# A conditioned decoder layer on one Trainium2 core: projections and copies reordered, a sort counted in two rows, and sums sent from the rows they end in

## The chip, the cores and the metric

The kernel runs on one core of a Trainium2 chip. Its time is the device time of the whole program in microseconds (us). Most runs of one kernel agree within 0.3%. The engines of a core work side by side, each through its own queue in order: TensorE (PE: matmuls, and PEld: the loading of their stationary operands), VectorE (DVE), ScalarE (ACT), GpSimd (POOL), and SyncE (SP), which here only starts DMA transfers. ACT and POOL also start transfers, and an engine that waits for a transfer or for another engine holds up all that is behind it in its queue.

## The reference

One layer of a decoder, run for a prompt of 512 tokens and for 8 samples of 8 tokens (64 tokens), 576 tokens of 2048 channels in all:

```python
h  = RMSNorm(x) * (1 + scale1) + shift1            # scales, shifts and gates from silu(c) @ w_ada
x_lru, y_gate, B, C, x_sc = split(h @ W_in)        # 5 x 1024 channels
a  = RGLRU(causal_conv4(x_lru)) * gelu(y_gate)     # recurrent scan, 16 heads of 64
b  = B * causal_conv3(C * x_sc)
x  = x + gate1 * (concat(rmsnorm(a), rmsnorm(b)) @ W_out)
h2 = RMSNorm(x) * (1 + scale2) + shift2
# PEER: 8 heads, 128 x 128 product keys, the best 16 of 16384 experts for each head
out[t] = sum over heads and picks of w * gelu(h2[t] . expert_u[e]) * expert_v[e]
x  = x + gate2 * out;   y = RMSNorm(x)
```

Outputs are y for both groups and the new states of the scan and of the two convolutions. All inputs are fp32.

## The kernel before

A product of two fp32 matrices is made of three matmuls of a rounded high part and a low remainder (`hi*hi`, `hi*lo`, `lo*hi`): the high part is written by ACT (`whi`, `xhi`, `hhi`), the low part by POOL or DVE (`wlo`, `xlo`, `hlo`).

First come the modulation and the first norm, then `project`, which streams a block of 128 output channels of a weight matrix in two halves of 8 x 128 rows and runs 96 matmuls of 288 tokens. The LRU loop goes over 8 channel groups: `lru_gate(i, 0)` and `lru_gate(i, 1)` are the small gate matmuls (`pg`), `lru` the scan. The products of the slices of `w_ada` that are needed later are put between as `ada_turn`. A second loop makes the projections c, s and b of the short convolution. `norm_stats` takes a norm: squares are summed by DVE (`sqa`), added over partitions by TensorE (`pc_g`), a root is taken by ACT and DVE (`rc`), and spread to all partitions by TensorE (`st_g`); the function it returns gives R. Then 16 projections with `w_out`, which read all of `hv`, the normed channels.

For h2, four quarters of four channel blocks are modulated, multiplied with the first block of the queries' weights (`qa`), transposed into a wide PSUM tile (`wide`, L609), and copied by ACT to `h2s` (L612); SP sends them to `h2d` in DRAM.

PEER is done in two ways at once. Experts that are picked by many tokens are computed densely: a list of 84 blocks of 128 experts is streamed, first `ut` (the U stream, 168 pieces of 24 matmuls, `pu`) and then `v` (the V stream, 84 steps of four columns, `pv`). Their activations weigh with a table that `gbank` matmuls build piece by piece from outer products of pairs (`op`, `wr`) that DVE and ACT make. Tokens that have many picks outside of the list are sorted by DVE and TensorE into tiles (`SORTED`: first position, 64 or 128 tokens, number of rows) with the samples' group 0 ahead. For each tile, rows of expert_u and expert_v are gathered by indirect DMAs that POOL starts (L1147), DVE takes dot products in the U stream (L1175), and adds rows times weights in the V stream into `accB` in PSUM (L1201). A tile of 64 tokens has two picks of each token beside each other, one on partitions 0 to 63 and one on 64 to 127, so its sum has two halves. ACT copies the sum to a new row buffer (L1205), and POOL adds it to `accd` in DRAM by one indirect DMA for 128 tokens or two, the second adding to the first, for 64 (L1210).

A planner in Python writes the order of the queues: before each piece, `ahead` takes steps of the generators as far as a credit in microseconds allows (a `yield 4.0` is a step that costs 4.0), and `LAG` says how many pieces behind the tile's rows its next stage begins. Row buffers are handed out by `new_row`, six in the V stream, in rotation. In the V stream each step's weights are split by ACT (L843) and POOL (L844). `finish_b` ends the samples' part: it reads their sums from `accd` (`tokb`), transposes them with 32 matmuls (`ph`, L1378), and writes y; `fplan` names the columns of the V stream between which its steps stand. At the end the four blocks of prompt tokens are read from `accd` (`tok`) and added by matmuls to the last group's sums.

Of the kernel before, what the change touches and what calls it, by code (L numbers as in the profile page):

```python
# [49 lines left out]
FULL_ROWS = 1.25  # L50
LAG = 2
PAIRS = 6
# [25 lines left out]
def build(ctx, tc, A, O, dbg=None):  # L78
# [36 lines left out]
    def stream_w(src, nm, share=8):  # L115
        his, los = [], []
        for hf in range(2):
            raw = ws.tile([128, 8, 128], F32, name=f"raw_{nm}_{hf}", tag="wraw", bufs=2)
            nc.sync.dma_start(raw, src[:, 8 * hf:8 * hf + 8, :])
            hi = ws.tile([128, 8, 128], F32R, name=f"whi_{nm}_{hf}", tag="whi", bufs=2)  # L120
            S.activation(hi, raw, AF.Copy)
            lo = ws.tile([128, 8, 128], F32R, name=f"wlo_{nm}_{hf}", tag="wlo", bufs=2)
            lo_engine(share).tensor_sub(lo, raw, r32(hi))
            his.append(hi)
            los.append(lo)
        return his, los

    def mm3(outs, his, los, movs, ks=range(KD)):
# [427 lines left out]
    R = spread()  # L556
# [46 lines left out]
    for q in range(4):  # L603
        modulate(x1, R, 4, 3, 4 * q, 4, "h2")
        mm3(pq0, *w_q, movs, range(4 * q, 4 * q + 4))
        for i in range(NA // 128):
            for k in range(4):
                for p in range(2):
                    PE.matmul(wide[:, i, k * 128:(k + 1) * 128], hv[p][:, 4 * q + k, i * 128:(i + 1) * 128], idr,  # L609
                              start=p == 0, stop=p == 1)  # L610
        t = adap.tile([128, 4, 512], F32, name=f"h2s{q}", tag="wa")
        S.activation(t, wide, AF.Copy)  # L612
        for i in range(NA // 128):
# [31 lines left out]
    actd = dr.tile([L, 128, NA], F32, name="actd")  # L645
    accd = dr.tile([T, D], F32, name="accd")
    x2d = dr.tile([128, KD, NA], F32, name="x2d")
# [116 lines left out]
    slot_of, row_log, slots_now = {}, [], [RB]  # L764

    def new_row(nm):

        k = len(row_log)
        s_ = slot_of[k] = (slot_of.get(k - 1, -1) + 1) % slots_now[0]
        row_log.append(False)  # L770
        return (gp if s_ < RB else pools["vx"]).tile([128, D], F32, name=nm, tag=f"row{s_}", bufs=1), k

    def row_free():

        s_ = (slot_of.get(len(row_log) - 1, -1) + 1) % slots_now[0]
        return all(row_log[k] for k in range(max(0, len(row_log) - 2 * RV), len(row_log)) if slot_of[k] == s_)

# [240 lines left out]
    def sort():  # L1018
# [12 lines left out]
        rk = pools["rsort"].tile([128, QT], F32, name="rk")  # L1031
        hot = []

        def count_up():
            for out, lhs, rhs, first, last in hot:
                PE.matmul(out, lhs, rhs, start=first, stop=last)  # L1036
            hot.clear()

        for z in range(QT):
# [3 lines left out]
            V.tensor_scalar(oh, io, rk[:, z:z + 1], None, op0=ALU.is_equal)  # L1043
            todo_ = []
            for i, (p0, n, c) in enumerate(GT):
                if p0 is None:
                    continue
                lhs = oh[:, p0:p0 + n]
                if n < 128:
                    lhs = pools["rsort"].tile([128, 128], F32, name=f"ohd{i}_{z}", tag="ohd", bufs=4)  # L1050
                    V.tensor_copy(lhs.rearrange("p (r t) -> p r t", t=n),
                                  oh[:, None, p0:p0 + n].to_broadcast([128, 2, n]))
                todo_.append((pt[:, 2 * i:2 * i + 2], lhs, m[:, 0:2, z], z == 0 and i == 1,
                              z == QT - 1 and i == len(GT) - 1))
            count_up()
            hot.extend(todo_)
            yield 4.0
        yield None
        count_up()
        srt = pools["rsort"].tile([128, len(GT), 2], F32, name="sorted")  # L1060
# [123 lines left out]
    def gather_v(i):  # L1184
# [7 lines left out]
        def add(j):  # L1192
            r, a = held.pop(j)
            row_log[a] = True
            if j == 0:
# [4 lines left out]
                return  # L1200
            V.scalar_tensor_tensor(st["a"], r, dots[i][:, j:j + 1], st["a"], op0=ALU.mult, op1=ALU.add)  # L1201

        def end():
            t, a = new_row(f"acc{i}")
            S.activation(t, st["a"], AF.Copy)  # L1205

            def out():
                row_log[a] = True
                for o in range(0, 128, n):
                    G.indirect_dma_start(out=accd, out_offset=bass.IndirectOffsetOnAxis(ap=tok[:n, i:i + 1], axis=0),  # L1210
                                         in_=t[o:o + n], in_offset=None, compute_op=ALU.add if o else ALU.bypass)
            after.append([gu[0] + 3, out])

        for j in range(c):
            fetches.append(lambda j=j: fetch(j))
            uses.append(lambda j=j: (add(j), end() if j == c - 1 else None))

# [150 lines left out]
    def finish_b():  # L1368

        r = new_row("tokb")[0]  # L1370
        nc.sync.dma_start(r[:NG], accd[NA:T, :])
        xt = new_row("x2b")[0]
# [4 lines left out]
        for k in range(KD):  # L1377
            PE.matmul(ph[:, k * NG:(k + 1) * NG], r[:NG, k * 128:(k + 1) * 128], ident[:NG, :NG], start=True, stop=True)  # L1378
        V.tensor_tensor(s4(t), s4(ph[:, :KD * NG].rearrange("p (k t) -> p k t", k=KD)), ctx_b(g2, slice(0, KD)), op=ALU.mult)
# [433 lines left out]
```

## Time and profile before

| what | value |
|---|---|
| median of 3 runs | 3400.45 us (3397.44 to 3406.22) |
| profiled execution | 3398.16 us, its span 3396.0 us |
| TensorE busy | 3183.6 us, 94% of the span |
| TensorE's mean granted clock | 0.963 of full speed |
| DVE, ACT, POOL busy | 2155.1, 1084.6, 1739.4 us |
| moved by DMA | 868.17 MB, mean 256 GB/s |
| stages, by the trace | LRU loop to 380 us, short convolution to 729, w_out to 970, h2 and queries to 1236, U stream to 2336, V stream 2346 to 3366 |

A row of the timeline gives the start, the duration, the engine, the line of the kernel, the operation, output and inputs with shapes, and in brackets how long the engine sat idle before it and what ended this. A row of the waits gives the engine and the group that waited, what it waited for, the total, how often, and the longest. Matmuls are pipelined, so one lasts longer than the distance to the next.

### The profile page before, as it was taken

The numbers are of one execution on the slowest core, as the hardware profiler recorded it, in microseconds if no ns is written. First come the engines' busy times: TensorE is split into PE (matmuls) and PEld (weight loads), VectorE is DVE, ScalarE is ACT, GpSimd is POOL, SyncE is SP. The second block draws the span as 40 slices with busy tenths as digits, with TensorE's granted clock in tenths as the row PEclk, the third lists the DMA queues.
The fourth block names the chain that finished last, engine by engine and source line by source line (L and its number), as shares of the span: only waits on it lengthen the run. The fifth ranks groups of instructions, "written<-read, shape, count | busy, mean of one in ns | idle before, by whom it ended". The sixth has DMA issues, their size and how long they took to land.

```text
span 3396.0 us, 47497 instructions
## 1 busy us (share of the span) xinstructions
PE 3183.6 (94%) x17641; PEld 2699.9 (80%) x17641; DVE 2155.1 (63%) x3246; ACT 1084.6 (32%) x1665; POOL 1739.4 (51%) x993
## 2 busy tenths in 40 slices
PE   5899999989979999998999999998999999899987
PEld 2588789889969998877888888876887777687776
DVE  5355522243346898877788986755666777677735
ACT  3244211132232222223555555532322222222122
POOL 4233233344333246664565665655766676666732
PEclk8899999999979999999999999998999999999998
DMA  9643456633432228986979898988999988898954
GB/s 338 230 143 132 164 200 214 211 120 130 136 137 71 69 94 285 313 301 240 352 278 373 336 355 324 357 326 337 374 365 330 355 312 295 304 361 295 361 160 148
DMA packets 304030, 868.17 MB, mean 256 GB/s; under 512 B 36618, under 2 KB 80522, under 8 KB 255658
## 3 DMA queue, kind: packets, MB, share of 16 engines
q1 hardware_dynamic: 165152, 390.35, 33.6%
q0 software_dynamic: 62896, 386.64, 29.4%
q10 hardware_dynamic: 75744, 88.09, 7.4%
q8 instruction: 139, 2.28, 0.3%
q14 instruction: 99, 0.81, 0.1%
HBM read 864.69 MB, written 68.90 MB: 275 GB/s over the span
## 4 chain that ended last, share of the span: by engine, by line
PE 51%; DMA 4%; issue 4%; DVE 2%; POOL 2%; ACT 0%; POOLq 0%; SPq 0%; ACTq 0%; DVEq 0%
PE pu L1295 24%; PE pv L1315 23%; PE gbank L1491 3%; DMA v<-v,rows 2%; POOL xlo L844 1%; DMA u<-u,rows 1%; POOL v L1147 1%; PE pv L1319 0%; DMA tok<-accd 0%; DMA raw<-v 0%; DVE kk L1115 0%; DVE acc L1677 0%; DMA h2r<-h2d,tok 0%; PE tokp L1036 0%; PE ph L1378 0%
## 5 line engine op out<-in xcount | busy, mean ns | idle before, releaser
L844 POOL TENSOR_TENSOR xlo<-raw,xhi 128x1024 fp32r<-128x1024 f32 x336 | 821.3, 2457 | 647.8 <-ACT xhi L843 642.9
L843 ACT ACTIVATE xhi<-raw 128x1024 fp32r<-128x1024 f32 x336 | 354.7, 1060 | 858.4 <-PE pv L1315 429.1
L1201 DVE SCALAR_TENSOR_TENSOR accB<-v,dots,accB 128x2048 f32<-128x2048 f32 x205 | 482.3, 2353 | 187.8 <-DMA v<-v,rows 184.9
L1175 DVE SCALAR_TENSOR_TENSOR u<-u,hT 128x2048 f32<-128x2048 f32 x211 | 477.9, 2284 | 189.8 <-DMA u<-u,rows 172.8
L1315 PE MATMUL pv<-ahi,xhi 128*128 128x512 f32 x1344 | 538.4, 401 | 22.6 <-DVE acc L1337 13.3
L1315 PE MATMUL pv<-ahi,xlo 128*128 128x512 f32 x1344 | 535.8, 399 | 23.2 <-POOL xlo L844 23.2
L1295 PE MATMUL pu<-hhi,xhi 128*128 128x512 f32 x1344 | 541.9, 403 | 2.2 <-ACT xhi L843 2.2
L1315 PE MATMUL pv<-alo,xhi 128*128 128x512 f32 x1344 | 532.5, 396 | 0.0
L1295 PE MATMUL pu<-hhi,xlo 128*128 128x512 f32 x1344 | 529.0, 394 | 2.2 <-POOL xlo L844 2.2
L1295 PE MATMUL pu<-hlo,xhi 128*128 128x512 f32 x1344 | 530.6, 395 | 0.0
L1315 PEld LDWEIGHTS pv<-ahi,xlo 128*128 128x128 f32 x1344 | 256.0, 191 | 87.2 <-POOL xlo L844 27.6
L1315 PEld LDWEIGHTS pv<-ahi,xhi 128*128 128x128 f32 x1344 | 256.3, 191 | 84.3 <-ACT xhi L843 15.4
L1315 PEld LDWEIGHTS pv<-alo,xhi 128*128 128x128 f32 x1344 | 256.4, 191 | 58.0
L1295 PEld LDWEIGHTS pu<-hhi,xlo 128*128 128x128 f32 x1344 | 254.1, 189 | 60.3 <-POOL xlo L844 3.1
L1295 PEld LDWEIGHTS pu<-hhi,xhi 128*128 128x128 f32 x1344 | 255.2, 190 | 54.8 <-ACT xhi L843 2.6
L1295 PEld LDWEIGHTS pu<-hlo,xhi 128*128 128x128 f32 x1344 | 254.8, 190 | 50.1
L1147 POOL DMA_INDIRECT v<-v,rows x211 | 240.9, 1142 | 60.2 <-issue 38.0
L1147 POOL DMA_INDIRECT u<-u,rows x211 | 216.1, 1024 | 72.1 <-DVE u L1175 33.8
L1491 PEld LDWEIGHTS gbank<-wr,op 128*128 128x128 f32 x1024 | 135.5, 194 | 30.6 <-ACT op L1485 14.1
L1485 ACT ACTIVATE op<-op,it 128x128 f32<-128x128 f32 x512 | 154.5, 390 | 15.1 <-DVE op L1477 15.1
L186 PE MATMUL ada<-wa,cpad 128*32 128x512 f32 x768 | 114.6, 701 | 41.5 <-DMA wa<-w_ada 41.4
L1491 PE MATMUL gbank<-wr,op 128*128 128x84 f32 x1024 | 132.7, 273 | 18.0 <-ACT op L1485 13.3
(477 smaller groups left out, 5491.4 us busy)
## 6 DMA issues: line engine op xcount, KB each, us to landing
wa<-w_ada SPq DMA_DIRECT2D x96, 1024.0 KB
raw<-ut SPq DMA_DIRECT2D x168, 512.0 KB
raw<-v SPq DMA_DIRECT2D x336, 256.0 KB
actd<-act ACTq DMA_DIRECT2D x84, 256.0 KB
gd<-stg ACTq DMA_DIRECT2D x64, 336.0 KB
actr<-actd ACTq DMA_DIRECT2D x21, 1024.0 KB
gsb<-gd ACTq DMA_DIRECT2D x21, 1024.0 KB
raw_o<-w_out SPq DMA_DIRECT2D x32, 512.0 KB
```

The costliest lines, as they stand in the source:

```text
L186: PE.matmul(acc[32 * g:32 * g + 32, :], cpad[:, 4 * kq + g, :], w[:, g, :], start=kq == 0, stop=kq == 3)
L843: S.activation(hi, raw, AF.Copy)
L844: G.tensor_sub(lo, raw, r32(hi))
L1147: G.indirect_dma_start(out=out, out_offset=None, in_=src, in_offset=bass.IndirectOffsetOnAxis(ap=idx, axis=0), bounds_check=NE * 128 - 1, ...
L1175: V.scalar_tensor_tensor(r, r, 1.0, st["h"], op0=ALU.mult, op1=ALU.mult, accum_out=dots[i][:, j:j + 1])
L1201: V.scalar_tensor_tensor(st["a"], r, dots[i][:, j:j + 1], st["a"], op0=ALU.mult, op1=ALU.add)
L1295: PE.matmul(pu, st[:, kk, :], movA[mv](k), start=k == 0 and a == 0, stop=k == KD - 1 and a == 2)
L1315: PE.matmul(pv, st, mv, start=first and j == 0 and a == 0, stop=last and not end and j == SG - 1 and a == 2)
L1485: S.activation(ops[:, j0 + j, :], ops[:, j0 + j, :], AF.Copy, scale=it[2][:, b * 4 + j:b * 4 + j + 1])
L1491: PE.matmul(pg[:, j * L:(j + 1) * L], ops[:, j0 + j, :], wr[:, j0 + j, :], start=True, stop=True)
```

## The change

- In the last round of the LRU loop an `ada_turn` and the first c projection stand between the two gate matmuls. In the second loop the s projection stands ahead of the norm's matmuls.
- `out_half` runs one half of a w_out projection. The first halves of the first two stand ahead of the second norm's sum and between that and its spread; the other halves come where the projections were.
- The copy of `wide` is in two halves, each at high priority as soon as two blocks are transposed.
- In the sort, counts are made as two rows of 512 positions, by one matmul for each block of 128 tokens with a two-column stationary operand, copied by ACT (`two`), and turned by small matmuls into `tokq`. The step's cost for the planner is 1.3 instead of 4.0.
- `LAG` is 3 instead of 2.
- `free_slot` gives the row that has been free for longest, in place of a rotation.
- The last addition of a tile writes its sum over the last gathered row; ACT's copy and its row go. Group 0 goes as one plain DMA of 128 rows to `accs`. Of the others, the first part is sent two uses later and the second half of a 64-token tile four further uses later.
- `finish_b` reads `accs` and adds the two halves in its matmuls by `both`, the sum of the two halves of the identity. Its steps stand later in the V stream.

```diff
-LAG = 2
+LAG = 3
...
+        else:
+            ada_turn(1)
+            pc0 = project(A["w_in"][24], "c0")
         lru_gate(i, 1)
         lru(i)
         gate(i)
-        ada_turn(1)
+        if i + 1 < KW:
+            ada_turn(1)
...
-        sc_c(i, project(A["w_in"][24 + i], f"c{i}"))
+        sc_c(i, project(A["w_in"][24 + i], f"c{i}") if i else pc0)
+        ada_turn(2)
+        sc_x(i, project(A["w_in"][32 + i], f"s{i}"))
         if i == 0:
             spread = norm_stats(st, W, "g0")
...
-        sc_x(i, project(A["w_in"][32 + i], f"s{i}"))
-        ada_turn(2)
...
+    def out_half(k, hf):
+        hi, lo = half_w(A["w_out"][k], f"o{k}", hf)
+        mm3([p_out[k][:, i, :HT] for i in range(2)], (hi, hi), (lo, lo), movs, range(8 * hf, 8 * hf + 8))
+
+    p_out = [pp.tile([128, 2, 512], F32, name=f"pp_o{k}", tag="pp") for k in range(2)]
+    out_half(0, 0)
     spread = norm_stats(st, W, "g1")
+    out_half(1, 0)
     ada_turn(2)
     R = spread()
...
-            p = project(A["w_out"][k], f"o{k}")
+        if k < 2:
+            out_half(k, 1)
+            p = p_out[k]
+        else:
+            p = project(A["w_out"][k], f"o{k}")
...
-        S.activation(t, wide, AF.Copy)
+            if i % 2:
+                with tc.high_priority():
+                    S.activation(t[:, i - 1:i + 1, :], wide[:, i - 1:i + 1, :], AF.Copy)
...
+    def free_slot():
+
+        free = [(held_by.get(s_, -1), s_) for s_ in range(slots_now[0]) if s_ not in held_by or row_log[held_by[s_]]]
+        return min(free)[1] if free else None
...
-            yield 4.0
+            last_oh.append(oh)
+            yield 1.3
+            if z:
+                PE.matmul(pt[0:2, :], m[:, 0:2, z - 1], last_oh[z - 1], start=z == 1, stop=False)
         yield None
-        count_up()
+        PE.matmul(pt[0:2, :], m[:, 0:2, QT - 1], last_oh[QT - 1], start=False, stop=True)
+        two = pools["rsort"].tile([2, NA], F32, name="two")
+        S.activation(two, pt[0:2, :], AF.Copy)
+        yield None
+        pt = pbank("g", "tokq", 2)
+        for i, (p0, n, c) in enumerate(GT):
+            for o in range(0, 128 if i else 0, n):
+                PE.matmul(pt[o:o + n, 2 * i:2 * i + 2], two[:, p0:p0 + n], ident[0:2, 0:2], start=True, stop=True)
...
-        def end():
-            t, a = new_row(f"acc{i}")
-            S.activation(t, st["a"], AF.Copy)
...
-            after.append([gu[0] + 3, out])
+            V.scalar_tensor_tensor(r, r, dots[i][:, j:j + 1], st["a"], op0=ALU.mult, op1=ALU.add)
+            row_log[a] = False
+
+            if not i:
+                after.append([gu[0] + 2, lambda: (row_log.__setitem__(a, True), G.dma_start(accs, r))])
+                return
+
+            def out(o):
+                row_log[a] = o + n == 128
+                G.indirect_dma_start(out=accd, out_offset=bass.IndirectOffsetOnAxis(ap=tok[:n, i:i + 1], axis=0),
+                                     in_=r[o:o + n], in_offset=None, compute_op=ALU.add if o else ALU.bypass)
+            for o in range(0, 128, n):
+                after.append([gu[0] + 2 + 4 * (o > 0), lambda o=o: out(o)])
...
-        nc.sync.dma_start(r[:NG], accd[NA:T, :])
+        nc.sync.dma_start(r, accs)
+        both = vp.tile([128, NG], F32, name="both")
+        V.tensor_add(both, ident[:, :NG], ident[:, NG:])
...
-            PE.matmul(ph[:, k * NG:(k + 1) * NG], r[:NG, k * 128:(k + 1) * 128], ident[:NG, :NG], start=True, stop=True)
+            PE.matmul(ph[:, k * NG:(k + 1) * NG], r[:, k * 128:(k + 1) * 128], both, start=True, stop=True)
...
-    fplan = {(last + 1, 2), (last + 2, 0), (last + 2, 2), (last + 2, 3), (last + 3, 1), (last + 3, 3)}
+    fplan = {(last + 1, 2), (last + 2, 3), (last + 3, 1), (last + 3, 3), (last + 4, 1), (last + 4, 3)}
```

More of the change, by code (lines that the diff above doesn't have):

```diff
@@ L115, in stream_w, with half_w @@
     def stream_w(src, nm, share=8):
[L116 to L125, printed above, removed]
-        return his, los
+        his, los = zip(*[half_w(src, nm, hf, share) for hf in range(2)])
+        return his, los
+    def half_w(src, nm, hf, share=8):
+        raw = ws.tile([128, 8, 128], F32, name=f"raw_{nm}_{hf}", tag="wraw", bufs=2)
+        nc.sync.dma_start(raw, src[:, 8 * hf:8 * hf + 8, :])
+        hi = ws.tile([128, 8, 128], F32R, name=f"whi_{nm}_{hf}", tag="whi", bufs=2)
+        S.activation(hi, raw, AF.Copy)
+        lo = ws.tile([128, 8, 128], F32R, name=f"wlo_{nm}_{hf}", tag="wlo", bufs=2)
+        lo_engine(share).tensor_sub(lo, raw, r32(hi))
+        return hi, lo
     def mm3(outs, his, los, movs, ks=range(KD)):
@@ L605, in build @@
         mm3(pq0, *w_q, movs, range(4 * q, 4 * q + 4))
+        t = adap.tile([128, 4, 512], F32, name=f"h2s{q}", tag="wa")
         for i in range(NA // 128):
@@ L645, in build @@
     actd = dr.tile([L, 128, NA], F32, name="actd")
-    accd = dr.tile([T, D], F32, name="accd")
+    accd = dr.tile([NA, D], F32, name="accd")
+    accs = dr.tile([128, D], F32, name="accs")
     x2d = dr.tile([128, KD, NA], F32, name="x2d")
@@ L773, in row_free @@
     def row_free():
-        s_ = (slot_of.get(len(row_log) - 1, -1) + 1) % slots_now[0]
-        return all(row_log[k] for k in range(max(0, len(row_log) - 2 * RV), len(row_log)) if slot_of[k] == s_)
+        return free_slot() is not None
     for i in range(RB):
@@ L1031, in sort @@
         rk = pools["rsort"].tile([128, QT], F32, name="rk")
[L1032 to L1037, printed above, removed]
+        last_oh = []
         for z in range(QT):
@@ L1200, in add @@
                 return
[L1201 to L1212 removed]
+            if j < c - 1:
+                V.scalar_tensor_tensor(st["a"], r, dots[i][:, j:j + 1], st["a"], op0=ALU.mult, op1=ALU.add)
+                return
[3 more added lines that the diff above has]
+                after.append([gu[0] + 2, lambda: (row_log.__setitem__(a, True), G.dma_start(accs, r))])
+                return
+            def out(o):
[4 more added lines that the diff above has]
+                after.append([gu[0] + 2 + 4 * (o > 0), lambda o=o: out(o)])
         for j in range(c):
             fetches.append(lambda j=j: fetch(j))
[L1216 removed]
+            uses.append(lambda j=j: add(j))
     UO = range(len(GT))
```

22 lines of the change are left out of this document (5 added, 17 removed).

## The prediction

> **What bounds the kernel now.** I read the page first, then the chain, the waits of TensorE, and the timeline of POOL, DVE and ACT around each of those waits.
>
> ```profile
> span 3396.0 us, 47497 instructions
> PE 3183.6 (94%) x17641; PEld 2699.9 (80%) x17641; DVE 2155.1 (63%) x3246; ACT 1084.6 (32%) x1665; POOL 1739.4 (51%) x993
> PEclk8899999999979999999999999998999999999998
> PE 51%; DMA 4%; issue 4%; DVE 2%; POOL 2%; ACT 0%; POOLq 0%; SPq 0%; ACTq 0%; DVEq 0%
> ```
>
> TensorE is busy for 94% of the span and holds most of the chain that names an engine. The change removes almost no matmul work, so it can win only what TensorE does not use: the idle 3396.0 - 3183.6 = 212.4 us, and the slow matmuls behind each hole, where the granted clock falls. The waits say which holes there are (total, count, longest):
>
> ```profile
> PE pv L1315 <- POOL xlo L844: 23.2, 8, 7.8
> PE gbank L1491 <- ACT op L1485: 13.3, 2, 9.3
> PE pv L1315 <- DVE acc L1337: 13.3, 9, 3.0
> PE pc_g L225 <- DVE sqa_g L217: 8.7, 2, 6.9
> PE wide L609 <- ACT h2s L612: 8.6, 1, 8.6
> PE tokp L1036 <- issue: 7.7, 1, 7.7
> PE ph L1378 <- DMA tokb<-accd: 6.7, 1, 6.7
> ```
>
> The change touches all seven, each in whole or in part.
>
> **V stream: sums written into their rows, halves of 64-token tiles apart, oldest free row.** This is half of the forecast. Timeline of POOL and TensorE around three sums, and one undisturbed window (its columns: length, PE busy and count, PEld, DVE, ACT, POOL, granted clock, DMA share, GB/s):
>
> ```profile
> 2606.01 1.87 POOL L1210 DMA_INDIRECT accd<-acc,tok  x1 [9.47 <-DMA accd<-acc,tok]
> 2633.88 0.80 PE L1315 MATMUL pv<-ahi,xhi 128*128 128x512 f32 x1 [3.04 <-DVE acc L1337]
> 2925.77 4.76 POOL L844 TENSOR_TENSOR xlo<-raw,xhi 128x1024 fp32r<-128x1024 f32 x2 [8.66 <-ACT xhi L843]
> 2933.28 0.93 POOL L1210 DMA_INDIRECT accd<-acc,tok  x1 [0.30 <-issue]
> 2944.46 1.47 POOL L1210 DMA_INDIRECT accd<-acc,tok  x1 [10.26 <-DMA accd<-acc,tok]
> 2948.36 0.80 PE L1315 MATMUL pv<-ahi,xlo 128*128 128x512 f32 x1 [7.80 <-POOL xlo L844]
> 2953.92 0.39 PE L1315 MATMUL pv<-ahi,xhi 128*128 128x512 f32 x1
> 3133.95 1.48 POOL L1210 DMA_INDIRECT accd<-acc,tok  x1 [10.67 <-DMA accd<-acc,tok]
> 3137.87 0.79 PE L1315 MATMUL pv<-ahi,xlo 128*128 128x512 f32 x1 [7.30 <-POOL xlo L844]
> 3158.78 0.50 PE L1315 MATMUL pv<-ahi,xhi 128*128 128x512 f32 x1 [0.68 <-DVE acc L1337]
> 2960.00:3130.00 170.00, 168.24 (x729) 136.36 (x728) 138.98 (x84) 41.00 (x37) 115.66 (x70) 1.00 0.93 344
> ```
>
> POOL issues the second half of a tile right behind the first, and sits some 10 us until the first has landed (it must: the second adds to the same rows). Its queue holds the next xlo, which TensorE wants. At 2948.36 that costs TensorE 7.80 us; then thirteen matmuls take 2953.92 - 2948.36 = 5.56 us where 168.24 / 729 = 0.231 us each would be 3.00, so 2.6 more: 10.4. The same reading gives 7.30 + about 2 = 9.3 at 3137.87, and 3.04 + about 3 = 6 at 2633.88, where POOL's lost time came out as late rows for DVE. Small waits just behind the three (0.4 to 1.9 us, eight of them, the last is the row at 3158.78) add about 6. Together 31.7 us.
>
> With the change the two halves are four uses of rows apart; in the built order one xlo pair and four fetches lie between: 4.76 + 4 x 1.3 (a fetch of 1.00 and its 0.30 of issue) = 10 us, against 2944.46 - 2933.28 = 11.2 us to land. So 1.2 us of 10.3 is left, at two tiles. The third stall, group 0, becomes one plain 128-row transfer with nothing behind it. POOL loses no instruction otherwise; ACT loses six copies, which lay beside TensorE: nothing. What is late next: the sum's row is now the oldest free one, so it is taken by the first or second fetch behind its transfer, and that fetch waits until it is read out: 11.2 - 1.0 - 4.76 = 5.4 us at most at the two 64-token tiles, up to 4 at the others. POOL has slack for that: it waited 8.66 us for xhi before its pair at 2925.77, so it runs ahead of TensorE there. I charge 3 us over all six sums (bounds 0 and 12: six times 2). Net +28.7, from 19 to 33.
>
> The Trainium skill, TensorE: Matmul & The Clock Gate, Part 1, says that after an idle window of about 3.4 us the array runs at half speed for about 3.4 us of busy time. Here the slow stretch behind the 7.80 us hole was 5.3 us or more; by the page each of three such holes would be worth about 1 us less, and the term about 26. The measurement decides.
>
> **End: finish_b later.**
>
> ```profile
> 3259.84 7.08 PE L1378 MATMUL ph<-ident,tokb 64*128 64x64 f32 x32 [6.68 <-DMA tokb<-accd]
> ```
>
> It now reads accs, written 600 us earlier instead of just now, so its 6.68 us go. The 32 instructions run at 7.08 / 32 = 0.22 us in the slow clock; at the full clock half, 3.5 us, and the V matmuls behind them are no longer slow (about 1). The stationary grows from 64 to 128 rows at the same moving width: nothing. The add that makes `both` is one small DVE instruction, beside other work. +11 (7 to 14). The last scatter is later used only by the four tok loads, as before.
>
> **First stages.** Timeline of TensorE, DVE and ACT, and a window of the h2 stage:
>
> ```profile
> 356.57 1.23 PE L432 MATMUL pg<-xc,g_lru_wa 64*64 64x300 f32 x8 [0.98 <-ACT ti L433]
> 362.88 2.27 PE L432 MATMUL pg<-xc,g_lru_wx 64*64 64x300 f32 x8 [5.08 <-ACT tr L433]
> 366.71 0.53 PE L136 MATMUL pp_c<-hhi,whi_c 128*128 128x288 f32 x2
> 379.32 0.43 PE L136 MATMUL pp_c<-hhi,wlo_c 128*128 128x288 f32 x2
> 381.55 1.28 PE L225 MATMUL pc_g<-ones,sqa_g 128*128 128x1 f32 x10 [1.80 <-DVE sqa_g L217]
> 735.53 2.26 PE L225 MATMUL pc_g<-ones,sqa_g 128*128 128x1 f32 x10 [6.85 <-DVE sqa_g L217]
> 742.16 2.28 DVE L558 SCALAR_TENSOR_TENSOR o<-o,cols,R_g 128x576 f32<-128x576 f32 x3 [2.91 <-ACT R_g L237]
> 754.02 2.62 DVE L243 TENSOR_TENSOR hlo<-o,hhi 128x576 fp32r<-128x576 f32 x2
> 990.46 0.48 PE L609 MATMUL wide<-idr,hhi 128*128 128x128 f32 x1 [8.65 <-ACT h2s L612]
> 1014.83 0.53 PE L136 MATMUL wide<-hhi,whi_q 128*128 128x288 f32 x1 [2.02 <-ACT h2s L612]
> 981.80:1018.40 36.60, 25.94 (x160) 25.79 (x160) 8.64 (x10) 13.57 (x13) 17.14 (x11) 0.72 0.41 144
> ```
>
> Last LRU round. A projection takes 379.32 + 0.43 - 366.71 = 13.0 us. c0 and an ada turn now lie in the 5.08 us wait; s0 takes c0's old place ahead of the norm and covers, as c0 did, the chain of 381.55 - 365.15 = 16.4 us from the last gate matmul to the squares. Gained: 5.08, the slow gate matmuls (2.27 against 1.23, so 1.04) and about 2 of the slow ada and st_g matmuls behind; the 1.80 stays. +8 (5 to 10).
>
> out_half. The first half of w_out[0], 6.5 us, fills the 6.85 us at 735.53. That of w_out[1] goes between pc_g and st_g, so R comes later, by about 6.5 less the two holes of 1.5 us and less slow clock: some 2.5 us, 742.16 to 744.7. From R, DVE with its helpers needs 754.02 + 2.62 - 742.16 = 14.5 us for the last eight chunks; the second half of o0 trickles behind them to about 760, and o1 ends near 766, where two whole projections from 744 with their waits ended it at about 770. The hole moves behind st_g rather than going: +3.5 (-1 to +7).
>
> h2 copies. The window has 10.7 us idle and a clock of 0.72. Half a copy now goes early on ACT; the other half still stands behind five of the next quarter's activations, so only the first half of quarter 1's transposes gets ahead of its wait, 2 to 3 us; each later quarter finds its copy done, the slow matmuls between 990 and 1002 shrink by about 2, and the 2.02 becomes about 1. +6 (0 to 10). SP sends the same h2d transfers; one weight load moves between two halves of them, read some 10 us later: nothing.
>
> **Sort and LAG.** Rows of the group view (min/median/max ns), of DVE, ACT and TensorE:
>
> ```profile
> L1036 PE MATMUL tokp<-nd_m,ohs x24: 251/353/353, 1524.0 to 1538.0; 128*128 128x2 f32 x24
> L1036 PE MATMUL tokp<-nd_m,ohd x16: 167/353/354, 1523.5 to 1538.2; 128*128 128x2 f32 x16
> 1564.78 0.83 DVE L1082 TENSOR_SCALAR sl<-R 128x128 uint32<-128x128 uint32 x1
> 1581.54 0.28 DVE L1115 MATCH_REPLACE8 kk<-sl,kk 128x128 f32<-128x128 f32 x1
> 1583.92 1.98 PE L1491 MATMUL gbank<-wr,op 128*128 128x84 f32 x8 [9.30 <-ACT op L1485]
> 1655.95 1.88 ACT L1162 ACTIVATE hT<-h2r 128x2048 f32<-128x2048 f32 x1 [10.41 <-DMA h2r<-h2d,tok]
> ```
>
> The counts took 40 small matmuls, about 40 x 0.19 = 7.6 us (they overlap by half). Now four with 512 moving columns: the gate row above moves 8 x 300 columns in 1.23 us, so 8 passes of 512 take 2.1, and seven transposes, about 3 to 4 in all. The 7.7 us wait for the first count stays: it is DVE's chain, and the first one-hot row comes no earlier. Eight copies go from DVE, one short copy comes to ACT: nothing. +1.5 (-2 to +4).
>
> The smaller cost told to the planner (1.3 for 4.0 of each count) and LAG 3 move DVE's work. Before, the lump of 1564.78 to 1581.82 (17.0 us, the first tile's top-k) ends just ahead of the pairs that gbank needs, and TensorE waits 9.30. In the built order the lump runs a piece later with the second tile's first steps behind it, about 28 us (the same instructions at the same durations, 17.0 + 11), and the first gbank one and a half pieces later. TensorE then reaches gbank three pieces of 5.5 = 16.5 us behind the lump's issue; the pairs are there after 3 for the row sums ahead, 28 and 2.1 (1583.92 - 1581.82): a wait of some 16.5, 7 worse. Against that, the second tile's h2r is fetched a piece ahead: ACT's 10.41 us at 1655.95, which holds xhi and lengthens two pieces by 5.0 and 2.1 (estimated from the starts of the U pieces), goes: 7 better. Net 0 (-10 to +8).
>
> **Sum.** V 28.7 + end 11 + LRU 8 + out_half 3.5 + h2 6 + sort 1.5 + U 0 = 58.7 us. The profiled execution took 3398.16 us (2.16 around its span), so 3339.5; the median of the runs shown, 3400.45, is 2.3 above it: **3342 us**.
>
> **The rivals.**
>
> DVE's lump decides (U). The wait at the first gbank is 20 to 30 us and the second tile's head start is used up by DVE, 63% busy over all and late for a few pieces. For it: 9.30 us waited there with a lump of 17.0. Against: the excess is DVE's, and pieces without sort work have DVE to spare. Loss 25 to 30 instead of 0: about 3370.
>
> The POOL wait moves instead of going. The fetch into the sum's row sits out the transfer, and the second half finds the first unfinished. For it: 11.2 us to land against 10 of work between, and in the built order the first fetch behind a 64-token tile's second half takes that very row. Against: the 8.66 us that POOL had in hand. If two thirds of the 31.7 come back: 3342 + 21 = 3363.
>
> The Trainium skill, DMA: Bandwidth & Descriptors, Rules for kernel authors, says of an accumulating DMA beside another access of the same bytes that one must wait for the earlier DMA's semaphore. The row at 2944.46 shows that wait; by this rule it cannot be dropped, only covered, and where the cover is short this rival holds.
>
> Slower: the same wait at all six sums, uncovered. Place: POOL, at the fetch behind each sum. Price: 10.4 us of TensorE each, as at 2948.36, and 2 of small waits: 6 x 12.4 = 74 against the 31.7 removed, 42 worse. With 11 + 8 + 3.5 + 6 + 1.5 = 30 from the other places and U at its bad end of -10: 3400 + 42 - 20 = 3422. It decides when more than four of the six sums stall in full ((31.7 + 20) / 12.4 = 4.2).
>
> The change does little. TensorE idles elsewhere for the same total: DMA, at a share of 0.93 in the undisturbed V window, has no more to give, and rows come late: 3392.
>
> **How the numbers follow.** Forecast 0.62, with its own range 3317 to 3362 (terms' ends, not all at once); the lump 0.12; the wait that moves 0.13; little 0.05; slower 0.08. The range 3315 to 3388 takes in the first three and leaves the last two and a few hundredths below. 0.3% of the time, 10 us, is what a measurement can tell: faster 0.87, same 0.05, slower 0.08.
>
> **What would show it.** In the waits of TensorE: xlo from 23.2 to under 10 in the V stream, no tokb wait, no 5.08 and no 6.85; h2s at 5 or less. At POOL: no wait of 9 us at a scatter, at the fetch behind it under 5. The first gbank's wait near 16 us, and the ACT wait for h2r gone. The prediction is wrong if POOL shows six waits of 8 us or more at v fetches with TensorE's waits behind them, if DVE's rows come late through several U pieces, or if V pieces still take their time with the DMA share at 1.

## The result, and the profile after

The changed kernel takes 3363.26 us (median of 4 runs, 3360.20 to 3368.04) against 3402.20 us: the ratio is 0.9887, with a 95% interval from 0.9867 to 0.9907. It is faster by 38.9 us, clear of the 10 us that a measurement can tell. The forecast was 58 us. The profiled execution took 3366.13 us, 32.0 less than the one before.

The page of the changed kernel:

```profile
span 3364.0 us, 47459 instructions
PE 3182.0 (95%) x17623; PEld 2695.6 (80%) x17623; DVE 2150.7 (64%) x3239; ACT 1077.9 (32%) x1666; POOL 1732.3 (51%) x992
PEclk8899999999989999998999999998999999999998
PE 49%; DMA 9%; issue 2%; DVE 2%; POOL 1%; ACT 0%; SPq 0%; POOLq 0%; DVEq 0%; ACTq 0%
```

TensorE was busy as long as before (3182.0 us against 3183.6): between these two profiles nearly all of the gain is idle time, as argued. Against a second profile of the kernel before (3188.1 us busy of 3398.8), 28.7 of the 34.8 us are idle time. The waits of TensorE in the changed kernel, those that answer to the ones shown before, and the new ones:

```profile
PE pv L1333 <- DVE acc L1355: 16.3, 8, 4.4
PE gbank L1511 <- ACT op L1505: 13.9, 1, 13.9
PE wide L626 <- ACT h2s L630: 8.8, 5, 4.1
PE tokp L1064 <- issue: 7.4, 1, 7.4
PE pv L1333 <- POOL xlo L867: 5.1, 3, 3.2
PE pp_o L136 <- ACT hhi L242: 3.9, 2, 3.6
PE st_g L233 <- DVE rc_g L146: 2.7, 1, 2.7
```

The V stream's wait for xlo went from 23.2 to 5.1 us; what is left stands at its start, between 2344 and 2365 us, none of it behind a sum. The wait for tokb (6.7) is gone, and the one for the squares fell from 8.7 to 0.4. But h2s still costs 8.8 us, in five parts, and DVE's acc rose from 13.3 to 16.3. One more wait shrank that no term of the prediction names, the one of the first V matmul, here before and after:

```profile
PE pv L1315 <- ACT xhi L843: 9.2, 1, 9.2
```

```profile
PE pv L1333 <- ACT xhi L866: 3.7, 1, 3.7
```

ACT's `xhi` stood behind its `ahi`, and that behind DVE's `actr`. Before, DVE waited for the activations to come back from DRAM; after, it did not. Why the transfer was in time is open. DVE before and after:

```profile
2340.68 2.29 DVE L1258 TENSOR_TENSOR actr<-actr,gsb 128x2048 f32<-128x2048 f32 x1 [5.67 <-DMA actr<-actd]
```

```profile
2336.95 2.28 DVE L1276 TENSOR_TENSOR actr<-actr,gsb 128x2048 f32<-128x2048 f32 x1
```

To see where the time went, the span is cut at starts of TensorE's groups. Each length is worked out from the first (or last) instruction of a group in the trace; `before` has two profiles, since the kernel was profiled again, and the last column holds the other runs whose code is the changed one in that stretch.

| stretch | before | changed | others like the changed |
|---|---|---|---|
| first gate matmul to end of the last b projection | 559.8, 560.2 | 554.2 | 552.6 to 555.4 |
| to the second norm's sum (all of w_out) | 221.2, 227.3 | 221.6 | 221.6 |
| first query matmul to first whole query projection (h2) | 45.2, 44.9 | 46.3 | 46.2 to 46.5 |
| to the U stream | 222.5, 222.4 | 223.8 | 223.5 to 224.0 |
| U stream, to the first V matmul | 1108.6, 1107.5 | 1106.9 | 1104.2 to 1109.5 |
| V stream, to the samples' matmuls (ph) | 913.9, 911.8 | 899.2 | 887.2 to 898.2 |
| ph to the last V matmul | 109.8, 111.7 | 95.9 | 95.4 to 97.9 |
| first V matmul to the 3696th | 906.9, 904.9 | 890.7 | 878.6 to 889.6 |
| from there to the last V matmul | 116.8, 118.6 | 104.5 | 103.9 to 106.4 |

The two rows that meet at ph do not hold the same work before and after: before, 3696 V matmuls stand ahead of ph and the first row ends with the 6.7 us wait for tokb; in the changed kernel 3732 do. The last two rows are cut at the same V matmul, so the gains of the V stream and of the end are read from them. Seven profiles share the V stream's code of the changed kernel (the changed one, and the six others in the row to the 3696th); they spread over 12 us, with a mean of 885.4, so a single profile tells little that is smaller. Below, "the V stream" is the row up to ph; among the changed kernel and those made from it that row holds the same work.

### The profile page after: what moved, and what is told of

Read it like the earlier page. It is cut to its first block, busy times and chain, and to the rows that moved or that the text cites. A ratio compares the mean times of both kernels' runs of the same rounds, so it can differ in the third digit from the quotient of the medians.

```text
span 3364.0 us, 47459 instructions
## 1 busy us (share of the span) xinstructions
PE 3182.0 (95%) x17623; PEld 2695.6 (80%) x17623; DVE 2150.7 (64%) x3239; ACT 1077.9 (32%) x1666; POOL 1732.3 (51%) x992
## 4 chain that ended last, share of the span: by engine, by line
PE 49%; DMA 9%; issue 2%; DVE 2%; POOL 1%; ACT 0%; SPq 0%; POOLq 0%; DVEq 0%; ACTq 0%
PE pu L1313 25%; PE pv L1333 20%; PE gbank L1511 3%; DMA gsb<-gd 2%; DMA v<-v,rows 2%; DMA actr<-actd 2%; DMA raw<-v 1%; DMA h2r<-h2d,tok 1%; POOL xlo L867 1%; PE pv L1337 0%; DMA tok<-accd 0%; DVE kk L1129 0%; DVE acc L1697 0%; DVE accB L1216 0%; POOL v L1161 0%
## 5 line engine op out<-in xcount | busy, mean ns | idle before, releaser
L1216 DVE SCALAR_TENSOR_TENSOR accB<-v,dots,accB 128x2048 f32<-128x2048 f32 x199 | 468.2, 2353 | 155.9 <-DMA v<-v,rows 149.0
L1333 PE MATMUL pv<-ahi,xhi 128*128 128x512 f32 x1344 | 536.8, 399 | 22.8 <-DVE acc L1355 16.3
L1355 DVE TENSOR_TENSOR acc<-acc,pv 128x512 f32<-128x512 f32 x144 | 96.8, 682 | 88.7 <-PE pv L1333 86.0
```

What stands on the lines that cost most here:

```text
L1333: PE.matmul(pv, st, mv, start=first and j == 0 and a == 0, stop=last and not end and j == SG - 1 and a == 2)
L1355: V.tensor_add(ak, ak, pv)
```

## The experiments

**Early half projections, and the pace of w_out.** In the first pair of profiles w_out looked as if out_half had won nothing (221.2 and 221.6 us), although o1 ended earlier: all later projections took 12.80 us instead of 12.48. So out_half was undone.

```diff
-    out_half(0, 0)
-    out_half(1, 0)
...
-        if k < 2:
-            out_half(k, 1)
-            p = p_out[k]
-        else:
-            p = project(A["w_out"][k], f"o{k}")
+        p = project(A["w_out"][k], f"o{k}")
```

> The changed kernel with the two early half projections undone, so that all 16 w_out projections run whole behind the norm. In the trace of the changed kernel the stretch from the last b projection's end to the second norm's sum (pc_n) takes 221.7 us against 221.2 before, although o1 ends 4.0 us earlier by that clock: the 14 projections behind it run at 12.80 us each instead of 12.48. Theory: the way the stream of w_out starts sets its pace (0.1300 or 0.1333 us a matmul) for all that follows without a hole. Then here it is 12.48 again and the stretch about 221 us. Rival: the pace is drawn anew in every execution, or belongs to other parts of the change; then 12.80 stays and the stretch takes 225 to 226 us.

It took 3370.67 us, at 12.80 us a projection: the rival's pace. The stretch took 227.3 us, a little beyond the rival's 225 to 226. Whether the pace belongs to other code or to the execution was left to two more runs. The kernel before, with only a comment added, profiled once more:

> The kernel before, profiled once more. Its first profile runs 15 projections of w_out at 0.1300 us a matmul (221.2 us from the last b projection to the norm); the same code in the run with only the later parts changed ran at 0.1333 (226.1 us). Theory: the pace is drawn by the execution; it may be 0.1300 or 0.1333 here, and 0.1333 (about 226 us) shows it. Rival: it belongs to the code of before; then 0.1300 and 221 us again. The V stream up to ph took 913.9 us: theory of the V holes, 910 to 918 again.

It took 3400.98 us. w_out ran at the slower pace, 227.3 us, and the V stream took 911.8 us. The window from 800 to 900 us, all of it w_out's matmuls (columns: length, PE busy and count, PEld, DVE, ACT, POOL, granted clock, DMA share, GB/s), first of the kernel before, then of the same kernel again:

```profile
800.00:900.00 100.00, 100.00 (x772) 100.00 (x771) 33.98 (x47) 27.38 (x32) 40.45 (x18) 1.00 0.41 133
```

```profile
800.00:900.00 100.00, 100.00 (x752) 100.00 (x751) 30.84 (x44) 26.82 (x32) 39.40 (x18) 1.00 0.41 132
```

The same code, the same granted clock and DMA load, and 772 against 752 recorded matmuls. So the pace does not belong to the code; whether the execution or the device it ran on sets it, the runs do not show. The profile that the prediction was made from had the fast one, 5 to 6 us better in this stretch than the others. Against the usual pace out_half won 227.3 - 221.6 = 5.7 us.

**The halves of the wide copy.** One copy for each quarter, as before:

```diff
-            if i % 2:
-                with tc.high_priority():
-                    S.activation(t[:, i - 1:i + 1, :], wide[:, i - 1:i + 1, :], AF.Copy)
+        S.activation(t, wide, AF.Copy)
```

> The changed kernel with one copy of the wide tile for each quarter, as before. From the first query matmul to the first whole projection the stage took 45.2 us before and 46.3 after. Theory: the halves cost about a microsecond, since the transposes of the second half wait for the copy of the first (4.1 us at the first quarter); here 45 us. Rival: the early copies help and something else in the changed kernel (the modulation, DMA) made the stage longer; then 48 us or more here.

The stage took 44.6 us and the stretch behind it 222.1, where the changed kernel has 46.3 and 223.8. The halves cost 1.7 us in each, about 3 together: the theory, with more than its one microsecond. The whole took 3363.21 us. The other way round, the second two blocks went to PSUM banks of their own and were copied one by one:

```diff
+        gs = [pbank("g", f"wg{q}_{i}", 2) for i in range(2)]
+        dst = [wide[:, 0, :], wide[:, 1, :], gs[0], gs[1]]
...
-                    PE.matmul(wide[:, i, k * 128:(k + 1) * 128], hv[p][:, 4 * q + k, i * 128:(i + 1) * 128], idr,
+                    PE.matmul(dst[i][:, k * 128:(k + 1) * 128], hv[p][:, 4 * q + k, i * 128:(i + 1) * 128], idr,
...
-            if i % 2:
+            if i:
                 with tc.high_priority():
-                    S.activation(t[:, i - 1:i + 1, :], wide[:, i - 1:i + 1, :], AF.Copy)
+                    S.activation(*((t[:, 0:2, :], wide[:, 0:2, :]) if i == 1 else (t[:, i, :], dst[i])), AF.Copy)
```

> The changed kernel with the transposes of blocks 2 and 3 written to two other PSUM banks, each a tile of its own, copied by itself as soon as it is full; blocks 0 and 1 stay in the wide tile. Theory: the wait is one of the tile as a whole; with tiles apart the 4.1 us go, later quarters wait under 1 us each, and the stage takes 38 to 41 us instead of 46.3, the whole kernel 5 to 8 us less. Rival: the stage is bound by the modulation on DVE and ACT or by ACT's queue; then 44 to 47 us.

It took 3348.57 us. The stage fell to 32.6 us, below what either theory gave. It is 17.6 us faster than the changed kernel's profiled execution: 7.3 of them lie in this stretch and the one behind it, and 8.6 in the V stream, whose code is the same and whose spread they are. Timeline of the changed kernel, its first copy on ACT and the transposes that waited:

```profile
975.21 1.00 ACT L630 ACTIVATE h2s<-wide 128x1024 f32<-128x1024 f32 x1
```

```profile
976.27 0.48 PE L626 MATMUL wide<-idr,hhi 128*128 128x128 f32 x1 [4.14 <-ACT h2s L630]
985.20 0.33 PE L626 MATMUL wide<-idr,hhi 128*128 128x128 f32 x1 [0.68 <-ACT h2s L630]
988.95 0.33 PE L626 MATMUL wide<-idr,hhi 128*128 128x128 f32 x1 [1.75 <-ACT h2s L630]
1000.16 0.33 PE L626 MATMUL wide<-idr,hhi 128*128 128x128 f32 x1 [1.11 <-ACT h2s L630]
1008.30 0.33 PE L626 MATMUL wide<-idr,hhi 128*128 128x128 f32 x1 [1.16 <-ACT h2s L630]
```

The first row waits inside quarter 0, with nothing of an earlier quarter in the tile: TensorE's transposes of blocks 2 and 3 stand until ACT has copied blocks 0 and 1, and this copy stood on ACT behind activations. The later waits, 0.7 to 1.8 us, are about as long as one copy. So two halves of one tile make TensorE wait for ACT within a quarter and again between quarters. With tiles apart the 4.14 us are gone, but part comes back in the query stage (230.2 instead of 223.8 us), where a new wait stands. ACT and TensorE of that run:

```profile
1004.10 0.41 ACT L891 ACTIVATE qt<-qa 128x288 f32<-128x288 f32 x1 [8.43 <-DMA h2d<-h2s]
```

```profile
1004.57 0.61 PE L136 MATMUL qa<-hhi,whi_q 128*128 128x288 f32 x1 [5.74 <-ACT qt L891]
```

ACT's first copy of the queries waits for the last h2d transfers. In the changed kernel it waits for them too, 4.7 us, but TensorE lost only 0.5 us by it, since it came later itself.

**POOL's waits at the rows of the sums.** POOL waited 26.5 us at fetches into rows that had just been sent. Timeline of POOL in the changed kernel, one at group 0 and one behind a 64-token tile (the longest, 8.8 us, stands behind the other):

```profile
2601.45 2.70 POOL L1161 DMA_INDIRECT v<-v,rows  x1 [7.62 <-DMA accs<-v]
2948.82 1.03 POOL L1161 DMA_INDIRECT v<-v,rows  x1 [6.50 <-DMA accd<-v,tok]
```

```diff
+    def sent(a):
+        s_ = next(s for s, k in held_by.items() if k == a)
+        held_by[s_] = len(row_log)
+        row_log.append(True)
...
-                after.append([gu[0] + 2, lambda: (row_log.__setitem__(a, True), G.dma_start(accs, r))])
+                after.append([gu[0] + 2, lambda: (G.dma_start(accs, r), sent(a))])
```

> The changed kernel, but a sum's row goes to the end of the line of free rows when it has been sent, so that the next fetches take other rows if any are free. POOL waited 26.5 us at four fetches for the transfers that read the sums (7.6, 3.6, 6.5, 8.8). Theory: these waits lie in POOL's slack, and TensorE's holes in the V stream (DVE acc 16.3 us) come from rows that land late for other reasons; then the V stream changes by less than 3 us. Rival: these waits delay the rows; then the acc waits at 2671, 2721 and 3000 us shrink, and the V stream is 8 to 14 us shorter.

It took 3360.17 us. None of those waits is left, and the V stream took 896.9 us, 2.3 less and within the spread: the theory's range. TensorE's waits for acc fell from 16.3 to 9.1 us, but those for xlo rose from 5.1 to 7.6 and the one for ACT's first sum from 2.2 to 3.7. As far as the time shows, the waits lay in POOL's slack.

**The halves, the copy and the row.** Three runs take the V stream's part to pieces. Both halves together again:

```diff
-                after.append([gu[0] + 2 + 4 * (o > 0), lambda o=o: out(o)])
+                after.append([gu[0] + 2, lambda o=o: out(o)])
```

> The changed kernel, but both halves of a 64-token tile's sum are sent two uses after the sum, one right behind the other. Theory: POOL waits some 10 us at each of the two second halves, and TensorE 7 us on xlo behind each plus a slow stretch: the V stream up to the samples' matmuls (ph) takes 899.2 us after, 891 to 899 in the other runs of the same code; here 908 to 920. Rival: what the change won in the V stream comes from the copy and the row that went away, not from the halves; then 891 to 902.

It took 3366.66 us, the V stream 901.9. That is below the theory's 908 to 920 and at the very end of the rival's 891 to 902. POOL waited 11.9 and 11.0 us at the second halves, but TensorE only 2.9 and 1.2 for the xlo behind them; 15 and 17 us later it waited 2.7 and 5.1 us for DVE's acc. POOL at the first of the two, then TensorE:

```profile
2921.45 1.78 POOL L1227 DMA_INDIRECT accd<-v,tok  x1 [11.88 <-DMA accd<-v,tok]
```

```profile
2927.01 0.79 PE L1333 MATMUL pv<-ahi,xlo 128*128 128x512 f32 x1 [2.85 <-POOL xlo L867]
2942.13 0.47 PE L1333 MATMUL pv<-ahi,xhi 128*128 128x512 f32 x1 [2.68 <-DVE acc L1355]
```

Whether the waits for acc belong to POOL's is not shown; the changed kernel has others of that size. Then the sum copied by ACT to a row of its own, with the changed times:

```diff
-            V.scalar_tensor_tensor(r, r, dots[i][:, j:j + 1], st["a"], op0=ALU.mult, op1=ALU.add)
-            row_log[a] = False
+            V.scalar_tensor_tensor(st["a"], r, dots[i][:, j:j + 1], st["a"], op0=ALU.mult, op1=ALU.add)
+            r, a = new_row(f"acc{i}")
+            S.activation(r, st["a"], AF.Copy)
```

> The changed kernel, but a tile's sum is finished in PSUM and copied by ACT to a row of its own, as before, and sent from there at the changed times. Theory: the copy and its row cost little by themselves, what the V stream won comes from the waits of POOL; then the V stream up to ph takes 891 to 900 us as in the other runs. Rival: the row that the copy takes is what made the gathered rows late and left POOL no lead; then 903 to 912 of the 913.9 before.

It took 3366.37 us, the V stream 896.8: the copy and its row are worth nothing that can be seen. And both at once, three uses after the sum (`gu[0] + 3` for both halves):

> The changed kernel with both the copy to a row of its own and the halves sent together, three uses after the sum, as before; what stays of the change in the V stream is group 0 as one plain transfer and the oldest free row. Up to ph the V stream took 913.9 and 911.8 us in two profiles of before, 899.2 in the changed one and 887 to 899 in the others of its family, 901.9 with the halves together, 896.8 with the copy. Theory: group 0's transfer and the choice of rows carry what the halves do not, some 10 us; then 899 to 905 here. Rival: copy and halves are only worth something together; then 909 to 915.

It took 3372.80 us, the V stream 906.2, between the theory's range and the rival's. Here the old holes are back. Its waits, and its two holes behind the second halves:

```profile
PE pv L1334 <- POOL xlo L867: 19.0, 4, 7.1
PE pv L1334 <- DVE acc L1356: 9.1, 6, 2.9
```

```profile
2934.61 0.80 PE L1334 MATMUL pv<-ahi,xlo 128*128 128x512 f32 x1 [7.13 <-POOL xlo L867]
3123.72 0.80 PE L1334 MATMUL pv<-ahi,xlo 128*128 128x512 f32 x1 [6.93 <-POOL xlo L867]
```

And the same two groups where only the halves are apart (the run with the copy):

```profile
PE pv L1334 <- DVE acc L1356: 16.8, 9, 3.0
PE pv L1334 <- POOL xlo L867: 5.9, 5, 3.2
```

Between these two runs only the times of the sends differ: both parts three uses after the sum in one, two and six in the other. xlo falls by 13.1 us and the V stream wins 906.2 - 896.8 = 9.4 us: this is what the halves are worth with the copy, by one profile each. acc rises by 7.7 here, but that is no effect that these runs can show: in the seven profiles of the changed V code acc takes 7.5 to 16.6 us, 13.2 on average, and the two profiles of before have 13.3 and 13.2. Up to the same V matmul it is 897.6 us here and 905.9 on average before; the 8.3 us stand with group 0's one transfer and the choice of rows, which were not taken apart.

**Rows fetched further ahead.** In the changed kernel DVE's waits for rows hold acc, and so TensorE. DVE, then TensorE:

```profile
2718.58 2.36 DVE L1216 SCALAR_TENSOR_TENSOR accB<-v,dots,accB 128x2048 f32<-128x2048 f32 x1 [9.11 <-DMA v<-v,rows]
2720.84 1.28 DVE L1355 TENSOR_TENSOR acc<-acc,pv 128x512 f32<-128x512 f32 x2
```

```profile
2721.67 0.77 PE L1333 MATMUL pv<-ahi,xhi 128*128 128x512 f32 x1 [4.42 <-DVE acc L1355]
```

The acc that would give a PSUM bank back stands in DVE's queue behind an addition whose row has not landed. Five rows ahead instead of four:

```diff
-            while gf[0] < min(len(fetches), gu[0] + (RB - 1 if slots_now[0] == RB else RV - 2), lim) and row_free():
+            while gf[0] < min(len(fetches), gu[0] + (RB - 1 if slots_now[0] == RB else RV - 1), lim) and row_free():
```

> The changed kernel with five rows fetched ahead in the V stream instead of four: of the six row buffers the copy's no longer takes one. DVE waits 149 us there for rows that land some 10 us after their fetch, and TensorE 16.3 us for DVE. Theory: the rows land late for want of distance; then the acc waits fall under 8 us and the V stream up to ph is 8 to 15 us shorter than 899.2. Rival: DMA has no more to give (share 0.9 to 1.0), or the sum's row blocks the fifth; then 890 to 900 as in the other runs.

It took 3362.89 us, the V stream 894.7, acc 9.2 us, and the wait for ACT's first sum 6.5 instead of 2.2: the rival's range. One more row of distance does not move the stretch. Whether DMA's load or the order of DVE's queue makes these holes is open.

**LAG, and the parts ahead of the V stream.** LAG back to 2:

> The changed kernel with LAG 2. Theory: LAG 3 wins nothing and loses nothing by itself (a longer wait at the first gbank, an earlier h2r for later tiles): the U stream takes 1106.9 us after (1104 to 1110 in other runs of that code) and 1108.6 before; here 1102 to 1112. Rival: the lump of DVE work without the extra piece of distance stalls the first gbank by 20 us or more; then 1115 or more.

It took 3358.84 us, the U stream 1106.3, the first gbank waited 16.6 us instead of 13.9. LAG by itself is worth nothing that one profile shows, as forecast. Then the LRU part, out_half, the halves of the copy, LAG and the cost of 1.3 all undone together:

> The changed kernel with the parts ahead of the V stream undone: last LRU round, out_half, the halves of the wide copy, LAG 2, cost 4.0 in the sort; the two-row counts, the rows, the sums and finish_b stay. Theory: from the first V matmul to the last it takes 995 us like the changed kernel (1023.7 before), 4 us either way; the whole kernel comes to about 3372. Its w_out projections are the code of before: if the pace of 0.1300 us a matmul belongs to that code they run at 12.48 us again; if it is drawn by the execution or by what lies elsewhere, 12.80, as in all five traces of kernels made from the changed one.

It took 3359.93 us where 3372 was expected, no more than the changed kernel's median: its V stream had 891.9 us, at the good end of the spread, and its U stream 1102.8, the first gbank's wait 10.9. From the first V matmul to the last it took 891.9 + 95.4 = 987.3 us, below the 991 to 999 expected. w_out was at the slow pace again, 226.1 us. By the stretches that no other part touches, the undone parts are worth 5.6 us (LRU), 4.5 (out_half), -2.3 (copies) and about -4 (U): near 4 us all together.

**A version that beats both.** The changed kernel with tiles apart in the h2 stage, LAG 2 and the old cost:

```diff
-LAG = 3
+LAG = 2
...
-            yield 1.3
+            yield 4.0
```

> The changed kernel with the two later blocks of the wide copy in PSUM banks of their own, LAG 2 and the sort's cost of 4.0. The tiles apart took 13.7 us from the h2 stage and gave 6.4 back in the query stage, where the next copy waits for the h2d transfers; LAG 2 with the old cost left the U stream at 1102.8 us. Theory: these add up, and it is 9 to 16 us faster than the changed kernel, 3347 to 3355 us. Rival: what the U stream wins goes to the first V steps and to waits for rows; then within 5 us of 3355 to 3360.

3346.54 us (median of 4 runs, 3342.65 to 3355.44), ratio to before 0.9841, interval 0.9816 to 0.9867. Its profile has 32.6 us in h2, 230.6 to the U stream, 1102.0 in the U stream and 887.2 in the V stream. It is 16.7 us below the changed kernel's median, just past the edge of the 9 to 16 expected; the two were not timed side by side, and share only the kernel before.

## Why the prediction was right, and where it was not

The bound, the sign and most places were right: what was won is nearly all TensorE's idle time, and most of it at holes that the waits had named. The sum of 58.7 us was half again as large as what came, and the measured 3363 us lies one above the forecast's own range, 3317 to 3362. By its terms, with the stretches of both profiles of before:

- **End, +11: right, 12.4 and 14.1** up to the last V matmul, cut at the same V matmul. finish_b's matmuls no longer wait for tokb and run at a granted clock of 1.00 instead of 0.50, 3.68 us for the 32 that had taken 7.08:

```profile
3241.38 3.68 PE L1398 MATMUL ph<-both,tokb 128*128 128x64 f32 x32
```

- **Last LRU round, +8: 5.7.** The 5.08 us wait went. The 1.80 became nothing, but st_g waits 2.7 us instead, since DVE now has the s projection's work ahead of the norm's root: the step "the 1.80 stays" looked at TensorE's queue and not at DVE's.
- **out_half, +3.5: 4.5 to 5.7 at the usual pace, -0.4 between the two profiles compared.** The hole moved behind st_g and shrank to 3.6 us, as described.
- **h2 copies, +6: wrong, about -3** (1.7 in the stage, 1.7 behind it, by the run with one copy). The failed step is "each later quarter finds its copy done". The second half's matmuls also wait for the first half's copy within a quarter, 4.14 us in quarter 0, a wait that the prediction did not have.
- **Sort and LAG, +1.5 in all: 1.7 and 0.7, by luck.** From the first U matmul to the last the changed kernel took 3.7 us longer (1099.4 and 1099.5 before, 1103.2, and 1100.4 to 1105.6 in the others with that code); with LAG 2 and the old cost it is 1098.2 and 1099.0 again, so the pair is worth about -4 rather than 0, by the run with LAG 2 alone (1102.6) mostly the cost. What made it up is the hole ahead of the first V matmul, 9.2 and 8.0 us before and 3.7 after, which the prediction did not count. The counts and the small matmuls behind them still took TensorE about 7.1 us where 3 to 4 were worked out: the first six of 512 columns came 0.85 us apart, at a granted clock of 0.55 behind the 7.4 us wait, and the last two 0.43. The first gbank waits 13.9 us where 16.5 were worked out. ACT's wait for h2r did not go but fell from 10.4 to 4.9 us, and it is 5.2 with LAG 2, so the head start that LAG 3 should give is not the reason.
- **V stream, +28.7: 16.2 and 14.2 between the profiles, some 20 against the mean of the seven.** The waits for xlo behind the sums went, as forecast (of the seven, one profile keeps 2.8 us), and the second halves wait for nothing where 1.2 us were left. What failed is the step that counts all holes behind POOL's stall as gone with it: some 7 of the 31.7 us (the 3.04 and four of the small waits) were waits for DVE's acc, and those did not go in sum; acc took 13.3 and 13.2 us before and 13.2 on average after, at other places. ACT's first sum adds a wait of 1.5 to 5.7 us. Over all, the waits in this stretch fell from 36 to 21 us on average.
- **V stream, what POOL's waits cost.** The price is not fixed: 9 to 11 us at a second half cost TensorE 6.5 to 7.8 us of xlo with the copy, and 11 to 12 cost 1.2 to 2.9 without it and sent one use earlier; that this goes by how far POOL is ahead at that place is a reading, not shown. The waits at fetches into sent rows were mostly longer than worked out (6.5 and 8.8 us at the 64-token tiles against 5.4 at most, 7.6 and 3.6 at two others against 4), but the charge of 3 us for them held within the spread: without them the V stream was 2.3 us shorter. The shorter slow stretch of the Trainium skill (TensorE: Matmul & The Clock Gate, Part 1) would have made this term 26; the measured size lies below both, for another reason, and tells nothing on it.

Of the rivals, the lump in the U stream and the slower one did not come. "The POOL wait moves" came in POOL's own waits (30.4 to 26.5 us) but not in TensorE's: that its 3363 us is the time measured is a coincidence, since without those waits the V stream is only 2.3 us shorter. The Trainium skill, DMA: Bandwidth & Descriptors, Rules for kernel authors, says that an accumulating DMA beside another access of the same bytes must wait for the earlier DMA's semaphore. The run with both together shows that wait at 11.9 and 11.0 us, and in the changed kernel the work between covers it.

## What to carry to other kernels

Before counting a hole as won, look at which engine ended it: here the waits that POOL's stall ended itself went, and those for DVE's acc nearby, whose queue held the needed step behind one that waited, stayed as large as before. Cut the stretches that you compare at the same instruction, or the work that moved across the cut is read as a gain. A copy in halves helps only if the halves are apart for whatever tracks the waits; look for the wait at the second half's first instruction in the built order. And profile the kernel before twice: a stretch that differs between two profiles of the same code is no effect of the change.

## What was not expected of the hardware

Long runs of matmuls of 288 columns went at one of two steady paces under a granted clock of 1.00: 0.1300 us a matmul in 15 projections of one profile of the kernel before, 0.1333 in the other profile of the same code and in the profiles of the changed kernel and of all 11 made from it, without a visible difference in DMA load. Each held until the stream of projections ended. What sets it is open; it is worth 5 to 6 us in this kernel's w_out alone.
